# Equal instead of unequal token pieces in the weight-stationary projections of a hybrid SSD and MLA step

## The chip, the cores and the metric

The kernel runs on one core of one Trainium2 chip. The metric is the device time of one execution, in microseconds, lower is better. The core's engines are named as in the profile: PE (TensorE, with PEld for its weight loads), DVE (VectorE), ACT (ScalarE), POOL (GpSimd) and SP (SyncE, which issues most DMAs here).

## The reference

One inference step of two layers, for 1024 prompt tokens and 8 x 8 sample tokens, 1088 tokens of width 1024 in all. The layers are a Mamba-2 SSD layer and a latent attention (MLA) layer, each as h = h + Mixer(RMSNorm(h)). Only the projections that read the normed tokens are touched by the change:

```python
def ssd_mixer(h, conv_buf, ssm_state, w_in, conv_w, ...):
    proj = jnp.einsum('btd,de->bte', h, w_in)          # 1024 -> 2048 + 4096 + 32
    z = proj[..., :SSD_D_INNER]
    xbc = proj[..., SSD_D_INNER:SSD_D_INNER + SSD_CONV_DIM]   # 4096 columns
    xbc, new_buf = causal_conv(xbc, conv_buf, conv_w, conv_b)
    xbc = jax.nn.silu(xbc.astype(F32))
    ...                                                # the scan, gated norm, w_out

def mla_project(h, pos, w_in, ...):
    proj = jnp.einsum('btd,de->bte', h, w_in)
    gate = proj[..., o3:]                              # 1024 columns
    ...
```

The first layer's 4096 columns that go to the convolution, and the second layer's 1024 gate columns, are computed with the weights stationary in PE and the tokens moving.

## The kernel before

**Precision and order.** Each float32 operand is split into a high and a low part, and a product is three matmuls: high x high, low x high, high x low (`pairs` in `proj_piece`). The normed tokens lie transposed in `xh` and `xl` (`hh` and `hl` in the second layer), 8 tiles of 128 features by 1088 tokens.

**Weight-stationary projections.** A block is 128 output columns. `proj_piece` computes one block for one piece of the tokens: 8 feature tiles x 3 matmuls = 24 matmuls accumulate in one PSUM buffer of the tag "pj", of which there are two, and `evac` copies the piece out on ACT. A block has three pieces, taken from the list `TG`. In the first layer `Group.block` does it for 4 blocks in each of 8 groups (32 blocks); its eviction `ev` copies the first two pieces into `raw` (L511) and splits the last one into its prompt tokens (L513) and the 64 sample tokens (L514). Then ACT and DVE do the convolution from `raw` (L524, L528). In the second layer `gate_block` does 8 blocks, evicted through SiLU into `gt` (L994). `TG` also sets the three token groups in which the rows are normed and transposed (`norm_rows`, `norm_cols`, 384, 384 and 320 tokens).

**Around them.** A group's `gates` (the tile `z`, matmuls `pz` at L101 with the tokens stationary) and the scan of the group before (`ssd_chunks` and `ssd_states`) are put between the pieces. In the scan, a chunk's transposes write `trp` (L597 to L600), `cb` is B times C (L628), `py` the product with the decay matrix M (L640), `st` the state. The sample states' product `pv` (L726) shares its PSUM buffer with `cb`; ACT copies half of it to `yo` (L728) and DVE adds the rest (L729). `conv_out` transposes the last conv inputs (`ctp`), and `ssd_dt` makes the step sizes (`dpa`, L410). At the end of the first layer `OutHalf.prep` reads rows of y back into `yta0`, `yta1`, ... (two tiles in turn, even and odd), DVE scales them (L821), PE transposes them into `ytpa` (L829), ACT and DVE split them into `yha` and `yla`, and `ssd_out` multiplies them by the output weights into `poa` (L101), which DVE adds to the residual `xra` (L857).

**What sets the order.** A scheduler lays out all engines' instructions by simulated times, with estimated durations, except where the code pins them; in the second layer's attention PE and POOL are laid out by hand. So the program that results is one fixed order for each engine, in which an instruction waits only for what it needs.

Of the kernel before, what the change touches and what calls it, by code (L numbers as in the profile page):

```python
# [26 lines left out]
HD = 64  # L27
G = 8
TG = [(0, 384), (384, 384), (768, 320)]
TILES = [(i * 128, 128) for i in range(8)] + [(1024, 64)]  # L30
RAW = 3 + SEQ + NB * (NT + 3)
QL, KVL, ROPE, NOPE = 512, 256, 32, 64
# [53 lines left out]
def mm3(nc, out, pairs):  # L86
    n = len(pairs)
    for i, (a, b) in enumerate(pairs):
        nc.tensor.matmul(out, a, b, start=(i == 0), stop=(i == n - 1))  # L89
# [15 lines left out]
def both(xh, xl, i, kk):  # L105
    t0, m = TILES[i]
    a = xh[:, kk, t0 : t0 + m]
    return (a, None, xh[:, kk, t0 : t0 + 128]) if m == 64 else (a, xl[:, kk, t0 : t0 + m], None)
# [111 lines left out]
def rstd_of(k, out, ssq, n):  # L220
    nc = k.nc
    nc.vector.tensor_scalar(out, ssq, 1.0 / n, EPS, op0=ALU.mult, op1=ALU.add)
    m, n = out.shape[0], int(np.prod(out.shape[1:]))
    e = k.nhalf[:m, :n]
    if len(out.shape) == 3:
        e = e.rearrange("p (a b) -> p a b", a=out.shape[1])
    return nc.gpsimd.tensor_tensor(out, out, e, op=ALU.pow)
# [15 lines left out]
def norm_rows(k, gi, load, pool, xbufs):  # L243
    nc = k.nc
    t0, n = TG[gi]
    idx = [i for i, (a, m) in enumerate(TILES) if t0 <= a < t0 + n]
    xs = []
# [3 lines left out]
    for j, i in enumerate(idx):  # L251
        m = TILES[i][1]
        xt = pool.tile([128, D], F32, tag="xt", name=f"xt{i}", bufs=xbufs)
        load(xt, i)
        sq = k.sqp(f"sq{i}")
        with k.tc.issue_after(k.cols[gi - 1][SQ[gi - 1] + j].ins) if gi else nullcontext():
            nc.scalar.activation(sq[:m], xt[:m], AF.Square, accum_out=ssq[:m, j : j + 1])
        xs.append((xt, m, TILES[i][0] - t0))
        k.pow = rstd_of(k, rs[:, j : j + 1], ssq[:, j : j + 1], D)
# [5 lines left out]
def norm_cols(k, gi, xs, wcol, hi, lo, psum):  # L265
    nc = k.nc
    t0, n = TG[gi]
    for d in range(8):
# [18 lines left out]
def norm_steps(k, load, wcol, hi, lo, pool, psum, steps, xbufs, before=None, after=None, tail=False):  # L287
# [6 lines left out]
    for gi in range(3):  # L294
# [13 lines left out]
        if tail and gi == 0:  # L308
            xr, m = k.hr[8]
            k.tc.keep_in_program_order(k.nc.gpsimd.dma_start(k.h_d[TILES[8][0] : T], xr[:m]))  # L310

# [7 lines left out]
def load_w(k, pool, src, nk, ncol, tag, bufs=3, raws=None, rbufs=2, eng=None, sub=0, late=None):  # L319
    raw = load_raw(raws or pool, nk, ncol, rbufs)  # L320
    k.lastload = k.nc.sync.dma_start(raw, src.rearrange("(k p) e -> p k e", p=128))
    hi = pool.tile([128, nk, ncol], F32R, tag=tag + "h", name=tag + "h", bufs=bufs)
    lo = pool.tile([128, nk, ncol], F32R, tag=tag + "l", name=tag + "l", bufs=bufs)
    if late is None:
        split(k, hi, lo, raw, eng, sub)
    else:
        late.append((hi, lo, raw))
    return hi, lo
# [9 lines left out]
def kslices(w, n):  # L338
    return [(w[0][:, kk], w[1][:, kk]) for kk in range(n)]


def proj_piece(k, psum, ws, xh, xl, ci, evac):
    nc = k.nc
    t0, n = TG[ci]
    p = psum.tile([128, 512], F32, tag="pj", name="pj", bufs=PB["pj"])
    pairs = []
    for kk, (hi, lo) in enumerate(ws):
        a, b = xh[:, kk, t0 : t0 + n], xl[:, kk, t0 : t0 + n]
        pairs += [(hi, a), (hi, b), (lo, a)]
    mm3(nc, p[:, :n], pairs)  # L350
    evac(ci, t0, n, p)
# [109 lines left out]
class Group:  # L461
# [34 lines left out]
    def block(self, bi, acc):  # L496
        k, g, nc, wp, rp, gp = self.k, self.g, self.k.nc, self.wp, self.rp, self.gp
        blk = (16 + g, 24 + g, 2 * g, 2 * g + 1)[bi]
        first = g == 0 and bi == 2
        with ExitStack() as es:  # L500
            if first:
                es.enter_context(k.tc.issue_after(k.cols[1][7].ins))
                es.enter_context(k.tc.issue_after(k.xl_dma.ins))
            ws = self.pre.pop(bi, None) or self.weights(bi)
        raw = rp.tile([128, RAW], F32, tag="raw", name=f"raw{g}{bi}", bufs=2)
        smp = raw[:, 3 + SEQ :].rearrange("p (b w) -> p b w", w=NT + 3)
        nc.gpsimd.memset(raw[:, 0:3], 0.0)

        def ev(ci, t0, n, p):
            if ci < 2:  # L510
                nc.scalar.copy(raw[:, 3 + t0 : 3 + t0 + n], p[:, :n])  # L511
            else:
                nc.scalar.copy(raw[:, 3 + t0 : 3 + SEQ], p[:, : SEQ - t0])  # L513
                nc.scalar.copy(smp[:, :, 3:], p[:, SEQ - t0 : n].rearrange("p (b w) -> p b w", w=NT))  # L514

        for ci in range(3):
            if ci == 2:
                nc.gpsimd.tensor_copy(smp[:, :, 0:3], k.convT[:, blk].rearrange("p (b w) -> p b w", w=3))
            proj_piece(k, self.psum, ws, k.xh, k.xl, ci, ev)
            yield  # L520
        nc.gpsimd.tensor_copy(self.ct[:, bi, 0:3], raw[:, SEQ : SEQ + 3])
        nc.gpsimd.tensor_copy(self.ct[:, bi, 3:].rearrange("p (b w) -> p b w", w=3), smp[:, :, NT:])
        n = RAW - 3
        nc.scalar.activation(acc, raw[:, 3:], AF.Identity, bias=k.convb[:, blk : blk + 1],  # L524
                             scale=k.convw[3][:, blk : blk + 1])
        for j in range(3):
            with k.tc.issue_after(self.conv.ins) if self.conv else nullcontext():
                last = nc.vector.scalar_tensor_tensor(acc, raw[:, j : j + n], k.convw[j][:, blk : blk + 1], acc,  # L528
                                                      op0=ALU.mult, op1=ALU.add)
        self.conv = last if g == 0 and bi == 0 else None  # L530
# [18 lines left out]
    def gates(self):  # L549
# [3 lines left out]
        self.z = []  # L553
        for i, (t0, m) in enumerate(TILES):
            if i % 5 == 0:
# [431 lines left out]
def gate_block(k, wp, raws, b):  # L987
    with k.tc.issue_after(k.gts[5].ins) if b in (3, 4) else nullcontext():
        ws = kslices(load_w(k, wp, k.I["mla_w_in"][0][:, 800 + 128 * b : 928 + 128 * b], 8, 128, "wg", 3, raws,
                            eng=k.nc.gpsimd, sub=4), 8)  # L990
    gt = wp.tile([128, T], F32, tag="gt", name=f"gt{b}", bufs=2)

    def ev(ci, t0, n, p):
        k.gts.append(k.nc.scalar.activation(gt[:, t0 : t0 + n], p[:, :n], AF.Silu))  # L994

    for ci in range(3):
        proj_piece(k, k.psum, ws, k.xh, k.xl, ci, ev)
        yield
    k.gst = k.nc.sync.dma_start(k.g_d[b], gt)

# [12 lines left out]
def mla_in(k, right, mid):  # L1013
    tc, nc, I = k.tc, k.nc, k.I
    k.g_d = k.dram.tile([8, 128, T], F32, name="g_d")
    with ExitStack() as st:
# [8 lines left out]
        with k.h0, open_pool(tc, name="h1", bufs=1, side="right") as p0:  # L1025
            k.gts = []
            tc.keep_in_program_order(nc.scalar.preload_act_table_set("silu_and_others"))
            first = [gate_block(k, wg, rw, 0), gate_block(k, wg, rw, 1)]
            norm_steps(k, h_loader(k), k.normc[1], k.xh, k.xl, p0, k.psum, first, 3, tail=True)
            for b in first:  # L1030
                next(b, None)
# [5 lines left out]
        def gate_steps():  # L1037
            for b in range(2, 8):
                for ci, _ in enumerate(gate_block(k, wg, rw, b)):
                    if b > 2:  # L1040
                        next(stage, None)
                    yield
# [1083 lines left out]
```

## Time and profile before

| | us |
|---|---|
| three runs | 1914.87, 1917.70, 1918.49 |
| median | 1917.7 |
| span of the profiled execution | 1915.0 |
| PE busy in it | 1887.4 |
| DVE, ACT, POOL busy | 1208.5, 1101.1, 823.3 |

The span is the profiled execution's time from its first to its last instruction; no other time is known of that execution. A busy PE means that some matmul is under way: matmuls overlap, so that their starts, and not their durations, tell the rate. "Idle before" is the time in which an engine had nothing under way, with the engine and line that ended it.

### The profile page before, as it was taken

How to read it: one execution, taken by the hardware profiler on the slowest of the kernel's cores; microseconds unless marked ns; L12 is line 12 of the kernel's file. 1: busy time of each engine (PE TensorE's matmuls, PEld its weight loads, DVE VectorE, ACT ScalarE, POOL GpSimd, SP SyncE). 2: the span in 40 equal slices, each digit the busy share in tenths (PEclk: the TensorE clock that was granted, in tenths of full speed). 3: DMA queues.
4: the chain of work that ended last, by engine and by line, in shares of the span. 5: the costliest groups of instructions: out<-in, count | busy, mean ns of one | idle time of the engine just before them, and what ended most of it. 6: DMA issues, size and time to landing. Idle time of an engine off the chain costs nothing.

```text
span 1915.0 us, 33672 instructions
## 1 busy us (share of the span) xinstructions
PE 1887.4 (99%) x12023; PEld 1728.1 (90%) x12023; DVE 1208.5 (63%) x2500; ACT 1101.1 (57%) x2528; POOL 823.3 (43%) x1116
## 2 busy tenths in 40 slices
PE   8999999999999999999999999999999999999998
PEld 7999999999999999888788998898888887888887
DVE  5557676757676767765534214566887878666665
ACT  6467666767666666732214323436777777755552
POOL 2447555555655555453004322103443434764551
PEclk9999999999999999999999999999999999999999
DMA  5223323332323232644424662233111112664451
GB/s 165 54 79 91 94 83 94 88 106 83 101 84 99 85 99 78 212 158 175 166 110 133 209 226 75 69 110 95 47 52 41 53 41 58 228 204 142 146 170 37
DMA packets 183967, 212.51 MB, mean 111 GB/s; under 512 B 19148, under 2 KB 147928, under 8 KB 182776
## 3 DMA queue, kind: packets, MB, share of 16 engines
q1 hardware_dynamic: 177304, 185.32, 31.1%
q0 software_dynamic: 6416, 24.91, 3.8%
q8 instruction: 95, 1.56, 0.3%
q14 instruction: 72, 0.59, 0.1%
q10 hardware_dynamic: 80, 0.13, 0.0%
HBM read 151.76 MB, written 58.52 MB: 110 GB/s over the span
## 4 chain that ended last, share of the span: by engine, by line
PE 90%; DMA 3%; DVE 3%; ACT 3%; issue 1%; POOL 0%; SPq 0%; POOLq 0%; DVEq 0%; ACTq 0%
PE pj L89 24%; PE pz L101 8%; PE pq L101 6%; PE pob L101 5%; PE p L101 5%; PE poa L101 4%; PE py L640 3%; PE sc L89 3%; PE o L89 2%; PE sc L1402 2%; PE o L1465 2%; PE o L1467 2%; PE st L1434 2%; PE st L1435 2%; PE st L1436 2%; PE o L1466 2%
## 5 line engine op out<-in xcount | busy, mean ns | idle before, releaser
L89 PE MATMUL pj<-xl,wih 128*128 128x384 f32 (+1 forms) x768 | 255.4, 333 | 0.0
L89 PE MATMUL pj<-xh,wih 128*128 128x384 f32 (+1 forms) x768 | 252.9, 333 | 1.2 <-ACT xh L276 0.8
L89 PE MATMUL pj<-xh,wil 128*128 128x384 f32 (+1 forms) x768 | 252.9, 329 | 0.0
L1448 POOL TENSOR_TENSOR tl<-P,th 128x384 fp32r<-128x384 f32 (+1 forms) x96 | 90.6, 944 | 232.3 <-ACT P L1446 186.6
L528 DVE SCALAR_TENSOR_TENSOR acc<-raw,vec,acc 128x1112 f32<-128x1112 f32 x96 | 141.6, 1476 | 15.3 <-ACT acc L524 14.4
L89 PEld LDWEIGHTS pj<-xh,wih 128*128 128x128 f32 x768 | 143.8, 188 | 2.6 <-ACT xh L276 1.4
L89 PEld LDWEIGHTS pj<-xl,wih 128*128 128x128 f32 x768 | 144.5, 188 | 1.0
L89 PEld LDWEIGHTS pj<-xh,wil 128*128 128x128 f32 x768 | 144.5, 188 | 0.5
L101 PE MATMUL pz<-wih,xh 128*128 128x256 f32 x504 | 143.3, 288 | 1.4 <-ACT z L569 1.4
L101 PE MATMUL pz<-wil,xh 128*128 128x256 f32 (+1 forms) x504 | 139.8, 283 | 0.0
L1445 ACT ACTIVATE th<-st 128x512 fp32r<-128x512 f32 x192 | 94.6, 493 | 66.6 <-PE st L1441 50.9
L101 PE MATMUL pz<-wih,xl 128*128 128x256 f32 x448 | 128.5, 287 | 0.0
L1733 POOL TENSOR_TENSOR kvl<-pgr,kvh 128x256 fp32r<-128x256 f32 x128 | 97.8, 791 | 70.6 <-ACT kvh L1731 70.3
L635 ACT ACTIVATE M<-M,tok 128x128 f32<-128x128 f32 (+1 forms) x288 | 90.4, 386 | 51.4 <-DVE M L631 51.2
L136 DVE TENSOR_TENSOR wil<-wraw,wih 128x512 fp32r<-128x512 f32 x88 | 74.4, 851 | 38.2 <-ACT wih L130 31.7
L101 PEld LDWEIGHTS pz<-wih,xh 128*128 128x128 f32 x504 | 95.9, 190 | 2.3 <-ACT z L569 1.8
L1446 ACT ACTIVATE P<-st 128x512 f32<-128x512 f32 x192 | 93.5, 487 | 0.0
L101 PEld LDWEIGHTS pz<-wil,xh 128*128 128x128 f32 (+1 forms) x504 | 92.8, 184 | 0.1
L101 PE MATMUL p<-w,oh 128*128 128x512 f32 (+3 forms) x304 | 88.8, 386 | 0.6 <-DVE h L1983 0.6
L616 POOL TENSOR_TENSOR xdd<-xsT,tok 128x256 f32<-128x256 f32 x64 | 50.0, 781 | 86.4 <-ACT xsT L602 83.3
L101 PEld LDWEIGHTS pz<-wih,xl 128*128 128x128 f32 x448 | 85.4, 191 | 0.7
L1448 DVE TENSOR_TENSOR tl<-P,th 128x512 fp32r<-128x512 f32 x96 | 72.1, 752 | 18.9 <-ACT P L1446 18.7
(830 smaller groups left out, 6212.5 us busy)
## 6 DMA issues: line engine op xcount, KB each, us to landing
wraw<-in_ssd_w_in SPq DMA_DIRECT2D x92, 256.0 KB
M<-acs_d SPq DMA_DIRECT2D x64, 256.0 KB
s<-in_state_ssm SPq DMA_DIRECT2D x32, 256.0 KB
y_d<-y SPq DMA_DIRECT2D x64, 128.0 KB
out_s_ssm<-s SPq DMA_DIRECT2D x32, 256.0 KB
q_d<-qt SPq DMA_DIRECT2D x32, 192.0 KB
qp<-q_d SPq DMA_DIRECT2D x8, 768.0 KB
wraw<-in_ssd_w_out SPq DMA_DIRECT2D x10, 512.0 KB
```

Of the source, the lines that this page charges most:

```text
L89: nc.tensor.matmul(out, a, b, start=(i == 0), stop=(i == n - 1))
L101: nc.tensor.matmul(o, a, b, start=(j == 0), stop=(j == len(ops) - 1))
L136: return (eng or nc.vector).tensor_tensor(lo, src, hi.bitcast(F32), op=ALU.subtract)
L528: last = nc.vector.scalar_tensor_tensor(acc, raw[:, j : j + n], k.convw[j][:, blk : blk + 1], acc, op0=ALU.mult, op1=ALU.add)
L616: nc.gpsimd.tensor_tensor(v3(xdd), v3(xsT), hb(2), op=ALU.mult)
L635: nc.scalar.activation(M[:m, h, :m], M[:m, h, :m], AF.Exp, bias=tk[:, 0, 4 * g + h : 4 * g + h + 1])
L640: nc.tensor.matmul(py[:m, h * 64 : h * 64 + 64], M[:m, h, :m], xsT[:m, h * 64 : h * 64 + 64], start=True, stop=True)
L1402: nc.tensor.matmul(ps[:, :n], qh[:96, 128 * i : 128 * i + 128], kh[:96, 512 * c : 512 * c + n], start=True, stop=True)
L1445: nc.scalar.activation(th[:, :n], ps[:, :n], AF.Exp, scale=SCALE)
L1446: nc.scalar.activation(P[:, :n], ps[:, :n], AF.Exp, scale=SCALE)
L1448: eng.tensor_tensor(tl[:, :n], P[:, :n], th[:, :n].bitcast(F32), op=ALU.subtract)
L1733: nc.gpsimd.tensor_tensor(rl[:, j], raw[:, j], rh[:, j].bitcast(F32), op=ALU.subtract)
```

## The change

`proj_piece` takes the list of pieces as an argument. The first layer passes `PG`, the gates pass `PG2`. The norm groups keep `TG`. The numbers of pieces, blocks and matmuls stay.

```diff
 TG = [(0, 384), (384, 384), (768, 320)]
+PG = ((0, 368), (368, 368), (736, 352))
+PG2 = ((0, 376), (376, 360), (736, 352))
...
-def proj_piece(k, psum, ws, xh, xl, ci, evac):
+def proj_piece(k, psum, ws, xh, xl, ci, evac, parts):
     nc = k.nc
-    t0, n = TG[ci]
+    t0, n = parts[ci]
...
-            proj_piece(k, self.psum, ws, k.xh, k.xl, ci, ev)
+            proj_piece(k, self.psum, ws, k.xh, k.xl, ci, ev, PG)
...
-        proj_piece(k, k.psum, ws, k.xh, k.xl, ci, ev)
+        proj_piece(k, k.psum, ws, k.xh, k.xl, ci, ev, PG2)
```

The list of instructions on each engine stays the same but for the widths; their order, which the scheduler makes, changes from the first block to the gates on all engines. It is untouched in the attention that follows. Three places, with the order before and after (the changed kernel's lines have numbers two higher, and names carry the number of the buffer).

*The end of the first layer, DVE.* Before; `yta1` and `yta2` are rows of y for the second and third token tile of the output projection, `wraw` its weights, and the names with 6 and 7 belong to the scans of the last two groups:

```order
L636 TENSOR_TENSOR M7_0_10410<-M7_0_10410,cb7_0_10408 128x512
L113 TENSOR_TENSOR z75_10203<-z75_10203,pz_10348 64x256
L821 TENSOR_SCALAR yta2_10705<-yta2_10705,yrsa_10323 128x256 x4
L663 TENSOR_TENSOR y6_8_10286<-y6_8_10286,z65_8883 64x256
L136 TENSOR_TENSOR BTl7_0_10397<-trp7_0_10390,BTh7_0_10396 128x128
L774 SCALAR_TENSOR_TENSOR xl_99<-wraw_10382,vec_154,xh_98 128x8x128
```

and eleven rows on from L821:

```order
L663 TENSOR_TENSOR y7_0_10429<-y7_0_10429,z70_9914 128x256
L821 TENSOR_SCALAR yta1_10512<-yta1_10512,yrsa_10323 128x256 x4
L136 TENSOR_TENSOR sl7_800_10465<-s0p7_800_10459,sh7_800_10464 128x512
L631 TENSOR_TENSOR M7_1_10562<-M7_1_10562,negu_69 128x512
L631 TENSOR_TENSOR M7_2_10647<-M7_2_10647,negu_69 128x512
L857 TENSOR_TENSOR xra0_10484<-xra0_10484,poa00_10486 128x512
```

After:

```order
L776 SCALAR_TENSOR_TENSOR xl_99<-wraw_10386,vec_154,xh_98 128x8x128
L700 TENSOR_TENSOR xf7_80_10447<-x3p7_80_10439,tok3_78 96x256
L823 TENSOR_SCALAR yta1_10512<-yta1_10512,yrsa_10323 128x256 x4
L633 TENSOR_TENSOR M7_1_10562<-M7_1_10562,negu_69 128x512
L705 TENSOR_TENSOR x37_80_10449<-xf7_80_10447,x37_80_10449 32x256
L708 TENSOR_TENSOR b37_80_10452<-x3p7_80_10439,b37_80_10452 32x128
L664 TENSOR_TENSOR y7_0_10429<-py7_0_10418,xD7_0_10406 128x256
L649 COPY S7_1_10427<-st7_0_10423 128x256
L138 TENSOR_TENSOR sl7_800_10465<-s0p7_800_10459,sh7_800_10464 128x512
L665 TENSOR_TENSOR y7_0_10429<-y7_0_10429,z70_9914 128x256
L823 TENSOR_SCALAR yta2_10705<-yta2_10705,yrsa_10323 128x256 x3
L859 TENSOR_TENSOR xra0_10484<-xra0_10484,poa00_10486 128x512
```

The scaling of yta2 moved from ahead of yta1 to behind it, and in SP's queue its read moved behind that of yta1 in the same way.

*The same stage, PE.* Before, from the last rows ahead of the transposes of yta0 to the first `poa` (between the two pieces stand eight more `pz` matmuls):

```order
L628 MATMUL cb6_8_10271<-xs60_8139 64x64
L829 MATMUL ytpa00_10334<-ident_58,yta0_10326 128x128 x4
L829 MATMUL ytpa01_10341<-ident_58,yta0_10326 128x128 x4
L101 MATMUL pz_10348<-wih_9898,xh_98 128x256
L101 MATMUL pz_10348<-wil_9899,xh_98 64x256
```

and at the end of that stretch:

```order
L101 MATMUL pz_10348<-wih_9910,xh_98 128x256
L640 MATMUL py6_8_10281<-xsT6_8_10267,M6_8_10273 64x64 x4
L628 MATMUL cb7_0_10408<-acc70_9057 128x128
L101 MATMUL poa00_10486<-xh_98,yha0_10332 128x512
L101 MATMUL poa00_10486<-xl_99,yha0_10332 128x512
```

After:

```order
L103 MATMUL pz_10348<-wil_9911,xh_98 64x256
L103 MATMUL pz_10348<-wih_9910,xh_98 128x256
L831 MATMUL ytpa00_10334<-ident_58,yta0_10326 128x128 x4
L831 MATMUL ytpa01_10341<-ident_58,yta0_10326 128x128 x4
L642 MATMUL py6_8_10281<-xsT6_8_10267,M6_8_10273 64x64 x4
L630 MATMUL cb7_0_10408<-acc70_9057 128x128
L103 MATMUL poa00_10486<-xh_98,yha0_10332 128x512
L103 MATMUL poa00_10486<-xl_99,yha0_10332 128x512
```

The transposes ytpa moved behind the eleven `pz` matmuls, so that only py and cb stand between them and the first poa.

*The end of the first block, ACT.* Before; `raw00` and `raw01` take the last pieces of the first two blocks, `wih_699` and `wih_1188` are high parts of the next weights:

```order
L276 ACTIVATE xh_98<-xtp2_7_498,vec_154 128x320
L513 COPY raw00_259<-pj_506 128x256
L514 COPY raw00_259<-pj_506 128x8x8
L513 COPY raw01_287<-pj_534 128x256
L514 COPY raw01_287<-pj_534 128x8x8
L524 ACTIVATE acc00_258<-raw00_259,vec_154 128x1112
L524 ACTIVATE acc00_258<-raw01_287,vec_154 128x1112
L130 CAST wih_699<-wraw_697 128x512
```

After:

```order
L278 ACTIVATE xh_98<-xtp2_7_498,vec_154 128x320
L132 CAST wih_699<-wraw_697 128x512
L515 COPY raw00_259<-pj_506 128x288
L516 COPY raw00_259<-pj_506 128x8x8
L515 COPY raw01_287<-pj_534 128x288
L516 COPY raw01_287<-pj_534 128x8x8
L526 ACTIVATE acc00_258<-raw00_259,vec_154 128x1112
L526 ACTIVATE acc00_258<-raw01_287,vec_154 128x1112
```

The cast of wih_699 moved ahead of the four copies out of PSUM. In the later groups the order differs from the one before in each, and groups 2 and 4 are now laid out alike, as are 3 and 5: between the last `pv` of a group and its last `cb` (chunk 7) stood 38 `pz` matmuls in groups 2 to 5, and stand 43 in groups 2 and 4 and 34 in groups 3 and 5. In groups 3 and 5 the first four matmuls of the next conv block (`pj`) now stand ahead of the transposes `trp` of the next group's first chunk, which stood ahead of them. `dpa` stands two `pj` matmuls later.

## The prediction

> **What bounds the kernel now.** I read the page first (busy times), then the busy times by stretch, the groups of instructions by form, the timeline of TensorE (PE) for the spacing of matmuls, and the waits of PE.
>
> ```profile
> span 1915.0 us, 33672 instructions
> PE 1887.4 (99%) x12023; PEld 1728.1 (90%) x12023; DVE 1208.5 (63%) x2500; ACT 1101.1 (57%) x2528; POOL 823.3 (43%) x1116
> ```
>
> PE is busy for 99% of the span, while the next engine, VectorE (DVE), is busy for 63%. So the time is the sum of PE's matmul spacings plus the little that it waits. The stretches below are the first layer's groups, its output projection, and the gates:
>
> ```profile
> 60.00:755.00 695.00, 692.00 (x5060) 681.39 (x5059) 463.41 (x744) 455.94 (x1119) 376.95 (x567) 1.00 0.30 88
> 755.00:1027.00 272.00, 268.75 (x1501) 225.61 (x1499) 150.56 (x288) 106.06 (x235) 78.52 (x105) 1.00 0.46 157
> 1027.00:1140.00 113.00, 112.22 (x702) 108.90 (x701) 31.72 (x53) 42.57 (x83) 38.28 (x53) 1.00 0.61 212
> ```
>
> The first number after the comma is PE's busy time. From 60 to 1140 us, where all the changed matmuls but the first few pieces stand, PE is busy for 1072.97 of 1080 us. No stretch here is held by a load or by another engine for long. The granted clock is 1.00 in all three.
>
> **The spacing of a matmul by its width.** The duration of one (0.34 us at 384 columns in the rows below) is a latency: matmuls overlap. What counts is from start to start, read in three clean runs, first and last row of each (start and duration in us):
>
> ```profile
> 1061.67 0.34 PE L89 MATMUL pj<-hl,wgh 128*128 128x384 f32 x1
> ...
> 1069.65 0.34 PE L89 MATMUL pj<-hh,wgl 128*128 128x384 f32 x1
> ...
> 1120.80 0.31 PE L89 MATMUL pj<-hh,wgh 128*128 128x320 f32 x1
> ...
> 1124.17 0.31 PE L89 MATMUL pj<-hh,wgl 128*128 128x320 f32 x1
> ...
> 385.89 0.28 PE L101 MATMUL pz<-wil,xh 128*128 128x256 f32 x1
> ...
> 390.21 0.28 PE L101 MATMUL pz<-wil,xh 128*128 128x256 f32 x1
> ```
>
> The runs hold 47, 24 and 37 matmuls, so 46, 23 and 36 spacings: 7.98/46 = 173.5 ns at 384 columns, 3.37/23 = 146.5 at 320, 4.32/36 = 120.0 at 256. The slope is (173.5 - 146.5)/64 = 0.422 ns a column above 320 and (146.5 - 120.0)/64 = 0.414 below: nearly a straight line, with a fixed part of some 11 ns a matmul.
>
> **Term 1, the matmuls: 0.** The number of matmuls stays and every three pieces still hold 1088 columns. By the line, 368 columns take 173.5 - 16 x 0.422 = 166.7 ns, 352 take 160.0, 376 take 170.1 and 360 take 163.4. Three pieces took 2 x 173.5 + 146.5 = 493.5 ns for each weight tile; now 2 x 166.7 + 160.0 = 493.4 in the first layer and 170.1 + 163.4 + 160.0 = 493.5 in the gates. The first layer has 32 blocks of 24 weight tiles, 768 such sums, and the gates 192. If the bend of the line (0.414 against 0.422) fell all on the new widths, a sum would move by 0.4 ns, so 0.4 us in all to either side. I take 0.
>
> **Term 2, the evictions: 0.** ScalarE (ACT) copies a piece out of PSUM; columns are minimum, median and maximum in ns:
>
> ```profile
> L511 ACT COPY raw<-pj x64: 454/479/503, 24.2 to 749.5; 128x384 f32<-128x384 f32 x64
> L513 ACT COPY raw<-pj x32: 355/367/391, 48.2 to 755.2; 128x256 f32<-128x256 f32 x32
> L514 ACT COPY raw<-pj x32: 209/221/249, 48.5 to 755.4; 128x64 f32<-128x64 f32 x32
> ```
>
> That is (479 - 367)/128 = 0.875 ns a column, so a 368 piece takes 465 ns and the last piece's prompt part, now 288 columns, 395. A block took 2 x 479 + 367 + 221 = 1546 ns and takes 2 x 465 + 395 + 221 = 1546. What hides it is the next piece in the other of the two "pj" buffers, 24 x 160 ns = 3.84 us of matmuls; without that cover the last piece's copies would cost 28 ns more a block, 0.9 us over 32 blocks. I take 0. The gates' SiLU evictions go the same way. Their last piece and the first layer's begin at column 736 instead of 768 and so also read 32 columns of the second norm group, which is transposed before the third: no new wait.
>
> **Term 3, the new order.** The scheduler moved instructions on every engine from the first block to the gates. Each keeps its kind and number, so what can move is PE's waiting. The waits of PE from 60 to 1140 us (total in us, times, longest; six of ten rows):
>
> ```profile
> PE pz L101 <- ACT z L569: 1.4, 2, 0.7
> PE cb L628 <- DVE yo L729: 1.1, 3, 0.4
> PE trp L597 <- DVE yla L136: 1.0, 1, 1.0
> PE ctp L536 <- POOL ct L522: 1.0, 1, 1.0
> PE poa L101 <- DVE xra L857: 0.6, 1, 0.6
> PE dpa L410 <- DVE dta L404: 0.5, 1, 0.5
> ```
>
> The six sum to 5.6 us, and the four others stand below dpa's 0.5 each, so the whole is 5.6 to 7.6 us; I go on with 6.6. No order can gain more than that here by taking waits away, but for shorter pauses that the overlap hides.
>
> *End of the first layer.* The rows of before:
>
> ```profile
> 796.34 1.61 DVE L821 TENSOR_SCALAR yta<-yta,yrsa 128x256 f32<-128x256 f32 x4 [1.88 <-DMA yta<-y_d]
> ...
> 804.50 1.61 DVE L821 TENSOR_SCALAR yta<-yta,yrsa 128x256 f32<-128x256 f32 x4
> ...
> 808.66 0.47 PE L101 MATMUL poa<-xh,yha 128*128 128x512 f32 x1 [0.59 <-DVE xra L857]
> ...
> 810.37 0.33 PE L597 MATMUL trp<-ident,acc 128*128 128x128 f32 x1 [1.01 <-DVE yla L136]
> ```
>
> DVE waits 1.88 us for a tile that it scales too early (yta2) and spends 1.61 us on it, then does yta1, and is late for PE twice, 0.59 + 1.01 us. After the change yta1 comes first, so DVE is up to 1.88 + 1.61 = 3.49 us less behind there: both waits go, -1.6 us at most, 0 at least if DVE falls behind elsewhere; I take the whole. Against it, the transposes ytpa of yta0 come later, with only py and cb between them and the first poa; before, 11 more matmuls (11 x 0.12 = 1.3 us) stood there. poa needs ACT's cast and then DVE's subtraction. Those may now show as a wait, 0 to 1.3 us, and I take 0.5. yta2 is read behind yta1 now, and its transposes stand behind most of the 48 matmuls of tile 1; nobody waits. Together -1.1.
>
> *cb in groups 2 to 5.* PE waits for the PSUM buffer that yo frees:
>
> ```profile
> 292.31 0.28 PE L101 MATMUL pz<-wil,xh 128*128 128x256 f32 x1
> 292.95 0.49 PE L628 MATMUL cb<-acc 128*128 128x128 f32 x2 [0.36 <-DVE yo L729]
> ```
>
> Beyond the overlap it is 292.95 - 292.31 - 0.12 = 0.52 us, since the gate matmul ahead would hold PE for 0.12, and it comes three times, in groups 2, 3 and 4. In groups 2 and 4 now 43 gate matmuls stand ahead of cb instead of 38, 5 x 0.12 = 0.6 us of cover, and ACT's copy of yo is no longer behind y's squares: both waits go, -1.0. In groups 3 and 5 there are 34, 0.5 us less cover, partly made good by the same move on ACT: +0.25 each. Bounds -1.6 (all three gone) and +1.0 (both longer by the full 0.5 us and nothing gone); I take -0.5.
>
> *dpa* stands two matmuls later: 2 x 0.167 of its 0.5 us wait, -0.3.
>
> *End of the first block.* ACT now casts the next weights ahead of the copies that free the first "pj" buffer:
>
> ```profile
> L130 ACT CAST wih<-wraw 128x512 fp32r<-128x512 f32 x92 | 55.9, 616 | 45.4 <-PE pj L89 30.0 <-DMA wraw<-in_ssd_w_in 15.3
> ...
> 48.22 0.37 ACT L513 COPY raw<-pj 128x256 f32<-128x256 f32 x1 [1.72 <-PE pj L89]
> ...
> 48.76 0.45 PE L89 MATMUL pj<-xh,wih 128*128 128x384 f32 x1 [0.29 <-ACT raw L514]
> ```
>
> ACT had been idle for 1.72 us, so a cast, of 616 ns by its group's row, fits if its weights have landed: 0, or +0.6 if they land late. I take +0.2.
>
> *Group starts.* In groups 3 and 5 the first four conv matmuls now follow the gates directly, ahead of the transposes, on weights that ACT and DVE have only just split. I take +0.3 for each, +0.6, between 0 and 1.2 (twice the 616 ns of a cast).
>
> The sum is 0 + 0 - 1.1 - 0.5 - 0.3 + 0.2 + 0.6 = -1.1 us: 1913.9 us against the profiled execution's span of 1915.0. The median of the three runs is 1917.7, 2.7 above that span, so the forecast for the median is 1916.6. That is no change that can be measured: 0.2%, 3.8 us, is about what the runs can tell from none.
>
> **Rivals.** (a) *The array works in blocks of 32 columns.* Every width of these projections was a multiple of 64 before, so no row above speaks against it. 368, 376 and 360 would cost as 384, and the sum of three would be 1120 columns: 32 x 0.422 = 13.5 ns for 960 sums, +13.0 us, 1930.7. It decides if the 368 rows start 173 ns apart and not 167. For blocks of 16 only the gates lose, 16 columns in 192 sums, +1.3 us. The Trainium skill's page "TensorE: Matmul & The Clock Gate" (Step-by-step: what each phase is for) says that one column of the moving operand enters each cycle, so that throughput follows the column count alone; by that rule this rival is impossible and term 1 stays 0. The trace agrees at 256, 320 and 384 columns, where the slope is even; no run here yet shows a width between. (b) *New waits.* The order was laid out by estimated times, and PE can arrive early at products of ACT and DVE all over the seven group changes: the longest wait of the kind (pz on ACT) is 0.7 us. One at each of the seven and at the layer's end would add 8 x 0.7 = 5.6 us: 1923. It needs six such waits beyond those of before to pass 0.2%. (c) *The waits go.* If the list above vanished whole, 6.6 us would go: 1911. It must lose more than half, 3.8 us, to be faster by 0.2%; the four places that I followed give 3.4 at their best, and ctp and pz, 2.4 us, are open.
>
> **Numbers.** The forecast has 0.54, (c) 0.25, (a) 0.05 and (b) 0.16. So faster 0.25, same 0.54, slower 0.21. The range reaches from 1908, (c) with some short pauses gone as well, to 1926, past (b); (a) is left out.
>
> **What would show it.** In the changed kernel's profile the 368 and 352 matmuls should start 167 and 160 ns apart, and ACT's copies of 368 and 288 columns take 465 and 395 ns. PE's waits on yla and xra should be gone, and the waits of cb be seen in groups 3 and 5 alone. PE's share should stay at 99%. Wrong would be a spacing off the line by 5 ns, which is worth 4 us and more, or waits of PE from 60 to 1140 us that sum to under 3 or over 10 us.

## The result: 1.26% slower, and the profile after

The changed kernel took 1940.98 us in the median (1937.54 to 1942.53, 4 runs) against 1916.28 us (1914.14 to 1918.49, 4 runs) for the kernel before: a ratio of 1.0126, 95% interval 1.0111 to 1.0140. The forecast was no measurable change, 1916.6 us, with 1926.0 as the upper end of the range, so it missed.

The first lines of the page of the changed kernel:

```profile
span 1935.8 us, 33636 instructions
PE 1896.0 (98%) x12023; PEld 1731.0 (89%) x12023; DVE 1199.9 (62%) x2500; ACT 1100.2 (57%) x2528; POOL 828.6 (43%) x1116
```

The span grew by 20.8 us, PE's busy time by only 8.6. The same three stretches as in the prediction, the first made 20 us longer and the others moved by as much (the same columns: length, then PE, PEld, DVE, ACT and POOL busy, clock, DMA share, GB/s):

```profile
60.00:775.00 715.00, 701.94 (x5093) 687.41 (x5092) 456.31 (x746) 457.68 (x1125) 388.10 (x571) 1.00 0.30 86
775.00:1047.00 272.00, 265.65 (x1460) 221.07 (x1459) 147.81 (x284) 102.73 (x227) 74.31 (x101) 1.00 0.48 157
1047.00:1160.00 113.00, 112.21 (x693) 108.89 (x692) 32.69 (x54) 42.82 (x80) 38.88 (x53) 1.00 0.61 208
```

In the first stretch, the groups of the first layer, PE is idle for 715.00 - 701.94 = 13.1 us, where it was 695.00 - 692.00 = 3.0. In the second, the output projection, it idles 6.4 us (3.3 before), in the gates 0.8 as before. The stretches are cut by time and don't hold quite the same matmuls (5093 for 5060 in the first). Followed by instruction, the last conv matmul starts 16.1 us later than before (at 769.50 for 753.40) and the last one of the output projection 20.7 us later (at 1046.48 for 1025.80). The clock is a rounded mean: it reads 1.00 in all three, but in the first it hides a short drop to half, which the last section shows. Which waits these are, from the waits of PE in the same range (total in us, times, longest):

```profile
PE st L91 <- POOL xddl L138: 8.9, 8, 2.5
PE cb L630 <- DVE M L638: 2.0, 1, 2.0
PE pv L728 <- DVE sl L138: 1.6, 4, 0.9
PE cb L630 <- DVE yo L731: 1.3, 3, 0.7
PE st L91 <- ACT xddh L132: 1.0, 2, 0.7
PE sn L735 <- POOL bb L710: 1.0, 2, 0.5
PE poa L103 <- ACT yha L132: 0.9, 1, 0.9
PE pv L728 <- ACT sh L132: 0.8, 1, 0.8
PE poa L103 <- DVE xra L859: 0.7, 1, 0.7
```

The first row was not in the list before at all: in the scan, PE waits for `xddl`, the low part of the decayed inputs, which POOL makes for the state product `st`. The waits leave out what the overlap hides. So I also added up, for each kind of matmul, the time from the start of the matmul ahead to its own start, over the whole execution: these sums grew by 20.8 us, `st` by 12.9, `pj` 4.1, `pv` 3.0, `cb` 2.8, and everything else together fell by 2.1.

**The largest place.** It comes three times alike, in chunk 5 of the scans of groups 1, 3 and 5. First POOL at this chunk of group 1 in the kernel before, by its timeline (start, duration):

```profile
270.89 1.13 POOL L616 TENSOR_TENSOR xdd<-xsT,tok 128x256 f32<-128x256 f32 x1 [1.37 <-ACT xsT L602]
271.98 0.61 POOL L626 TENSOR_TENSOR xD<-xsT,dsk 128x256 f32<-128x256 f32 x1
272.55 0.73 POOL L136 TENSOR_TENSOR xddl<-xdd,xddh 128x256 fp32r<-128x256 f32 x1
```

DVE beside it, in the same timeline:

```profile
270.17 1.38 DVE L528 SCALAR_TENSOR_TENSOR acc<-raw,vec,acc 128x1112 f32<-128x1112 f32 x1 [0.84 <-ACT acc L524]
271.58 0.28 DVE L729 TENSOR_TENSOR yo<-yo,pv 32x128 f32<-32x128 f32 x1
271.88 0.69 DVE L735 TENSOR_TENSOR s<-s,sn 128x512 f32<-128x512 f32 x1
...
273.29 1.35 DVE L528 SCALAR_TENSOR_TENSOR acc<-raw,vec,acc 128x1112 f32<-128x1112 f32 x1
```

POOL at this chunk in the changed kernel's timeline:

```profile
269.46 1.34 POOL L618 TENSOR_TENSOR xdd<-xsT,tok 128x256 f32<-128x256 f32 x1 [1.66 <-ACT xsT L604]
270.77 2.11 POOL L628 TENSOR_TENSOR xD<-xsT,dsk 128x256 f32<-128x256 f32 x1
272.84 2.03 POOL L138 TENSOR_TENSOR xddl<-xdd,xddh 128x256 fp32r<-128x256 f32 x1
```

DVE beside it:

```profile
267.65 0.28 DVE L731 TENSOR_TENSOR yo<-yo,pv 32x128 f32<-32x128 f32 x1
267.96 0.69 DVE L737 TENSOR_TENSOR s<-s,sn 128x512 f32<-128x512 f32 x1
268.96 1.38 DVE L530 SCALAR_TENSOR_TENSOR acc<-raw,vec,acc 128x1112 f32<-128x1112 f32 x1 [0.32 <-ACT acc L526]
...
271.05 1.35 DVE L530 SCALAR_TENSOR_TENSOR acc<-raw,vec,acc 128x1112 f32<-128x1112 f32 x1
272.33 0.67 DVE L638 TENSOR_TENSOR M<-M,cb 128x512 f32<-128x512 f32 x1
272.93 1.36 DVE L530 SCALAR_TENSOR_TENSOR acc<-raw,vec,acc 128x1112 f32<-128x1112 f32 x1
```

And PE, which had come to this matmul at 272.4:

```profile
274.93 0.58 PE L91 MATMUL st<-xddl,BTh 128*128 128x256 f32 x1 [2.39 <-POOL xddl L138]
```

Before, DVE's two operations `yo` and `s` (0.97 us) stood between the first and the second step of a convolution, and POOL did xD and xddl in that gap, in 0.61 and 0.73 us. In the new order `yo` and `s` go ahead of the first step. The steps move together, and xD and xddl each fall on one: 2.11 and 2.03 us for the same work. Each ends about half a microsecond after the step beside it (272.88 after 272.40, 274.87 after 274.29), as if it did next to nothing while the step ran. Over all 192 operations of this kind (xdd, xD, xddl), 57 now stand beside a convolution step and take 43.8 us more than alone; before, 41 took 26.7 us more.

The Trainium skill, "SBUF — State Buffer" (SBUF: two separate sides; Who interferes with whom), says that a DVE instruction with two inputs in SBUF and a GpSimd instruction that reads SBUF contend for one shared read port, as an exclusive lock: whichever starts first gets it for the whole instruction, and the other fully blocks. The convolution step (raw and acc) has two such inputs, and the rows agree. They do not agree with the page's sentence that whoever starts first gets the port: by the profile xD started 0.28 us ahead of its step, and it was xD that stood. Whether the recorded start is the start of POOL's reads is not known.

**A wait of another kind.** `cb`'s 2.0 us for M comes in the scan of the last group, which runs beside the output projection. M stands on DVE behind the scaling of a tile of y, and DVE had idled 2.51 us for the read of that tile:

```profile
877.85 1.97 DVE L823 TENSOR_SCALAR yta<-yta,yrsa 128x256 f32<-128x256 f32 x4 [2.51 <-DMA yta<-y_d]
879.74 0.68 DVE L638 TENSOR_TENSOR M<-M,cb 128x512 f32<-128x512 f32 x1
```

### The profile page after: what moved, and what is told of

Read it like the earlier page. It is cut to its first block, busy times and chain, and to the rows that moved or that the text cites. A ratio compares the mean times of both kernels' runs of the same rounds, so it can differ in the third digit from the quotient of the medians.

```text
span 1935.8 us, 33636 instructions
## 1 busy us (share of the span) xinstructions
PE 1896.0 (98%) x12023; PEld 1731.0 (89%) x12023; DVE 1199.9 (62%) x2500; ACT 1100.2 (57%) x2528; POOL 828.6 (43%) x1116
## 4 chain that ended last, share of the span: by engine, by line
PE 82%; DMA 5%; ACT 4%; DVE 3%; POOL 3%; issue 2%; SPq 0%; POOLq 0%; DVEq 0%; ACTq 0%
PE pj L91 20%; PE pz L103 7%; PE pq L103 6%; PE pob L103 5%; PE p L103 5%; PE poa L103 4%; DMA M<-acs_d 3%; PE sc L91 3%; PE o L91 2%; PE py L642 2%; PE sc L1404 2%; PE o L1467 2%; PE o L1469 2%; PE st L1436 2%; PE st L1438 2%; PE st L1437 2%
## 5 line engine op out<-in xcount | busy, mean ns | idle before, releaser
L91 PE MATMUL pj<-xl,wih 128*128 128x368 f32 (+1 forms) x768 | 255.6, 333 | 0.0
L91 PE MATMUL pj<-xh,wih 128*128 128x368 f32 (+1 forms) x768 | 254.1, 335 | 1.3 <-ACT raw L516 0.7
L91 PE MATMUL pj<-xh,wil 128*128 128x368 f32 (+1 forms) x768 | 253.7, 330 | 0.0
L138 DVE TENSOR_TENSOR wil<-wraw,wih 128x512 fp32r<-128x512 f32 x88 | 70.5, 806 | 50.8 <-ACT wih L132 50.3
```

Of the source, the lines that this page charges most:

```text
L138: return (eng or nc.vector).tensor_tensor(lo, src, hi.bitcast(F32), op=ALU.subtract)
```

## The experiments

Theory A: the new order costs the time, above all by POOL's work standing beside DVE's convolution steps (A1). Theory B: the widths themselves cost it. An order can be kept while widths change, because every piece lies in a PSUM buffer of 512 columns: the program is laid out with one list of pieces, and then the operands of the 2880 matmuls and the copies out of PSUM are given other offsets and lengths in place.

**Old order, new widths, and the reverse.**

```diff
+    recut(nc, OLD, NEW)      # after the layout: pj matmuls and evictions get new offsets and widths
     r = run_bass_kernel_spmd(nc, [arrays], core_ids=[0])
```

> The order of the kernel before on every engine, with the new widths put in place of the old ones (368, 368, 352 and 376, 360, 352). Theory A, the new order costs the time: only the spacing of the matmuls is left. In the changed kernel three pieces of the first layer take 2 x 167.7 + 162.6 = 498.0 ns for a weight tile against 2 x 174.5 + 146.5 = 495.5 before, and of the gates 502.2 against 494.4, so 768 x 2.5 + 192 x 7.8 = 3.4 us: 1916.3 + 3.4 = 1919.7 us, and PE waits for st on POOL's xddl nowhere for over 0.5 us. Theory B, the widths cost the time (evictions and matmuls that don't fit each other any more): about 1941 us, with the order of before.

> The order of the changed kernel on every engine, with the old widths (384, 384, 320 in both layers). Theory A, the new order costs the time: 1941.0 - 3.4 = 1937.6 us, the waits of st on xddl stay at 2.4 to 2.7 us in three places. Theory B, the widths cost it: about 1916 us.

| | widths before | widths after |
|---|---|---|
| order before | 1 | 1919.76 us, 1.0005 (0.9994 to 1.0016) |
| order after | 1939.75 us, 1.0121 (1.0101 to 1.0140) | 1940.98 us, 1.0126 (1.0111 to 1.0140) |

Ratios are to the kernel before in the same session, which took 1918.56 us beside the two new cells and 1916.28 beside the changed kernel. The order alone makes 1.21%, the widths alone +0.05% (1.0 us, between -1.1 and +3.1), which is no difference that can be told. The first of PE's waits with the old widths in the new order shows the same place:

```profile
PE st L91 <- POOL xddl L138: 8.5, 5, 2.5
```

Theory B has fallen. Theory A's 3.4 us for the spacing lies just above the upper end of what was measured, 3.1: 1919.7 us was met, but beside a kernel before that took 1918.56 and not 1916.3.

**POOL without the steps beside it.** The nine steps at the three places, cut to 64 columns, so that this part of the convolution is left out:

```diff
+    narrow(nc)               # after the layout: acc<-raw steps of raw23, raw43, raw63: 1112 -> 64 columns
     r = run_bass_kernel_spmd(nc, [arrays], core_ids=[0])
```

> The changed kernel and its order; nine steps of the convolution on DVE (three each of the last blocks of groups 2, 4 and 6, which run beside POOL's work for chunk 5 of the scans of groups 1, 3 and 5) work on 64 of their 1112 columns, so that part of the convolution is left out. Theory A1, POOL is slowed by DVE's work beside it: xddl of these three chunks takes 0.73 us instead of 2.03, and xD 0.61 instead of 2.11; the three waits of PE for st, 2.5 us each, go: 1941.0 - 7.5 = 1933.5 us. Theory A2, POOL gets its input late, or is held by its own queue: its two operations keep 2 us each and the time stays at 1941.

Measured: 1933.19 us, ratio to before 1.0076 (1.0058 to 1.0095). POOL's timeline at the same place:

```profile
269.88 0.61 POOL L618 TENSOR_TENSOR xdd<-xsT,tok 128x256 f32<-128x256 f32 x1 [1.66 <-ACT xsT L604]
270.45 0.62 POOL L628 TENSOR_TENSOR xD<-xsT,dsk 128x256 f32<-128x256 f32 x1
271.02 0.74 POOL L138 TENSOR_TENSOR xddl<-xdd,xddh 128x256 fp32r<-128x256 f32 x1
```

The operations take 0.62 and 0.74 us again although POOL waits as long for its first input (1.66 us for xsT, as in the changed kernel), and the time fell by 7.8 us, or 9.6 by the ratios (1.0126 to 1.0076), where the three waits are worth 7.5 from start to start. Between the two profiles the sum for `st` fell by just these 7.5 us. A2, late inputs or POOL's own queue, has fallen: the steps beside them make the slowness.

**xddl ahead of xD.** The same three places with the two exchanged in POOL's queue, and nothing left out:

```diff
 L618 xdd1_5<-xsT1_5,tok
+L138 xddl1_5<-xdd1_5,xddh1_5
 L628 xD1_5<-xsT1_5,dsk
-L138 xddl1_5<-xdd1_5,xddh1_5
```

> The changed kernel and its order, except that in chunk 5 of the scans of groups 1, 3 and 5 POOL does xddl ahead of xD, for which PE doesn't wait. Theory A1 (POOL slowed by DVE beside it, and xddl behind a slowed xD): xddl starts when ACT's xddh is there, 271.25 instead of 272.84 us, and still takes about 2.0, so it ends some 1.6 us earlier; three waits of 2.5 us become 0.9: 1941.0 - 4.8 = 1936.2 us. If xddl's place behind xD doesn't matter, the time stays at 1941.

Measured: 1932.81 us, 1.0074 (1.0056 to 1.0092), 8.2 us less than the changed kernel (10 by the ratios) where 4.8 were expected. POOL's timeline:

```profile
271.20 1.67 POOL L138 TENSOR_TENSOR xddl<-xdd,xddh 128x256 fp32r<-128x256 f32 x1 [0.52 <-ACT xddh L132]
272.84 1.81 POOL L628 TENSOR_TENSOR xD<-xsT,dsk 128x256 f32<-128x256 f32 x1
```

Both are still slow, but xddl ends at 272.87 instead of 274.87 us, a little earlier than expected (1.67 and not 2.0 us), and no wait of st for POOL is over 0.6 us now. From start to start `st` lost 5.1 us between the two profiles, near the 4.8 expected. The rest was not traced; some 4 us of it can be the granted clock, whose median over the runs is 0.998 here and 0.996 in the changed kernel (the last section has the estimate). So the place of a slowed operation that nobody waits for, ahead of one that PE waits for, made most of those waits.

**How much of the whole is POOL beside DVE.** All 96 convolution steps on DVE cut to 64 columns, in the changed kernel and in the kernel before, so that most of the convolution is left out of both:

```diff
-                        getattr(a, "memref", "")[:6] in ("raw23_", "raw43_", "raw63_") for a in i.ins):
+                        getattr(a, "memref", "").startswith("raw") for a in i.ins):
```

> The changed kernel and its order; all 96 steps of the convolution on DVE work on 64 of their 1112 columns, so that most of the convolution is left out and DVE has some 100 us less to do. Theory P, POOL slowed by these steps is the main cost of the new order: beside the 7.5 us of the three places, the three half-microsecond waits for xddl in chunk 4 and the 0.9 us wait in group 7 go, and this kernel comes within some 5 us of the next one (the order of before, cut alike): about 1925 us or less. Theory R, the rest of the loss is waits of another kind (pv on DVE's sl, cb on DVE's M and yo, which only follow from what stands ahead of what): it stays at 1929 to 1933 us, over 10 us above the next one.

> The kernel before and its order, with the same 96 steps cut to 64 columns. It is the floor to compare with: PE has few waits there, and those for DVE and POOL (cb on yo 1.1 us, ctp on POOL 1.0, the steps' end) can shrink: 1914 to 1919 us by both theories.

Measured: 1926.06 us, 1.0047 (1.0030 to 1.0065), and 1915.47 us, 0.9991 (0.9981 to 1.0001). The two orders lay 24.7 us apart and now lie 10.6 us apart in one session. So the steps account for some 14 us of the loss, 7.5 of it at the three places; the rest, 10.6 us, is of another kind: with the steps cut, xdd, xD and xddl take only 0.6 us in all more beside them than alone. Some 3 us of it can be the granted clock (0.9975 in the median against 0.999; estimate in the last section). Neither theory hit: P gave 5 us, R over 10 with the time at 1929 or more. What remains of PE's waits in the changed order, the first rows:

```profile
PE st L91 <- ACT xddh L132: 1.8, 3, 1.2
PE cb L630 <- DVE M L638: 1.5, 1, 1.5
PE pv L728 <- DVE sl L138: 1.5, 4, 0.7
```

These look like waits that follow from what stands ahead of what on ACT and DVE; none of them was tested. From start to start the two profiles differ by 12.6 us, with `st` 4.8, `pj` 3.6 (the spacing of the new widths among it), `pv` 1.8 and `cb` 1.2. Cutting the steps also frees DVE of some 100 us, so the 14 us are not the contention's alone. What makes up the rest stays open.

**Another order for nearly the same work.**

```diff
-PG = ((0, 368), (368, 368), (736, 352))
-PG2 = ((0, 376), (376, 360), (736, 352))
+PG = ((0, 384), (384, 352), (736, 352))
+PG2 = TG
```

> Other widths in the first layer (384, 352, 352; the gates as before), and the order that the scheduler makes for them. In that order DVE's s and yo stand again between two convolution steps ahead of chunk 5 in every group, as in the kernel before, and the third step stands later. Theory A1: xD and xddl of chunk 5 then take 0.6 to 1.1 us and no wait of 2.5 us for st remains: at most 1941.0 - 7.5 = 1933.5 us, and down to 1918 if nothing else was lost. If the widths that differ from multiples of 64 were to blame, it would be near 1941 like the changed kernel.

Measured: 1923.35 us, 1.0031 (1.0017 to 1.0046), as A1 expected (at most 1933.5); xD and xddl of chunk 5 take 0.61 and 0.74 us in groups 1 to 5. Of the waits for xddl, 0.9 us are left, two of at most 0.6; `cb` on M, 2.0 us, stays. Pieces that differ from the changed kernel's by 16 columns in the first layer, and by 8 to 32 in the gates, gave an order 17.6 us better, and one that is still slower than the one before.

**The mend in the source, for both kernels.** The code holds xD behind xddl in the first and last group. Held in all:

```diff
-        with k.tc.issue_after(behind.ins) if not smp and g in (0, G - 1) else nullcontext():
+        with k.tc.issue_after(behind.ins) if not smp else nullcontext():
```

> The changed kernel with xD held behind xddl in all groups in the source (so far in the first and the last alone), and the order that the scheduler then makes. On DVE the three convolution steps now lie around chunk 5's xdd, xD and xddl in all five groups 1 to 5, without s and yo between, as in groups 1, 3 and 5 of the changed kernel. If it is the place of xddl behind a slowed xD that counts, no wait of st passes 1 us and the time is 1928 to 1935 us, as with the three exchanged by hand (1932.8). If a crowded DVE costs by itself, five places instead of three cost 2.5 us each: 1941 + 5 = 1946 us.

> The kernel before with xD held behind xddl in all groups in the source, in the order that the scheduler then makes. DVE has s and yo between the convolution steps in all five groups, and PE waits for xddl nowhere there, so there is nothing to win: 1914 to 1920 us. If the wait for xddl is what a scheduler's new order puts in by chance, it can be slower, up to 1925.

Measured: the changed kernel with it 1941.37 us, 1.0123 (1.0106 to 1.0140); the kernel before with it 1921.48 us, 1.0018 (1.0008 to 1.0028). The first is a miss. The single waits for xddl came out nearly as expected, none over 1.1 us where 1 us was the bound, but the scheduler made a new order around the pin, with more waits of the other kinds. The first rows of PE's waits:

```profile
PE st L91 <- POOL xddl L138: 4.6, 7, 1.1
PE cb L630 <- DVE yo L731: 4.0, 6, 0.9
PE pv L728 <- DVE sl L138: 3.9, 9, 0.7
PE st L91 <- ACT xddh L132: 3.8, 6, 0.7
```

An exchange by hand in a standing order gained 8 us; the same exchange given to the scheduler as a rule gained nothing, since all else moved too. In the kernel before, where no such wait was to be had, the rule lost 0.2%.

**The widths in one sweep.** The order of before, with the 32 blocks cut in 16 ways:

> The order of the kernel before; the 32 blocks of the first layer are cut in 16 different ways (two blocks each), with pieces of 288 to 512 columns, and the gates in 376, 360, 352. By the straight line of the prediction (11 ns + 0.422 ns a column) the matmuls start 139.5 ns apart at 336, 156 at 344, 160 at 352, 163 at 360, 167 at 368, 170 at 376, 180 at 400, 187 at 416, 200 at 448. By the spacing that the changed kernel shows (352 at 158 or at 167 in different runs, 360 at 166.4, 376 at 173), widths that are no multiple of 64 lie 1 to 3 ns above the line, and multiples of 64 on it. By blocks of 32 columns, all widths from 353 to 384 would take 173.

One run, 1923.82 us. Mean spacing between neighbouring matmuls of one width (longer pauses left out; 13 of the 27 widths), against the prediction's line:

| columns | 320 | 336 | 344 | 352 | 360 | 366 | 368 | 376 | 384 | 386 | 400 | 416 | 448 |
|---|---|---|---|---|---|---|---|---|---|---|---|---|---|
| line, ns | 146 | 153 | 157 | 160 | 163 | 166 | 167 | 170 | 173 | 174 | 180 | 187 | 200 |
| measured, ns | 146.2 | 153.3 | 157.8 | 162.2 | 166.4 | 166.8 | 168.1 | 173.2 | 174.8 | 178.3 | 180.7 | 188.3 | 202.8 |

The block rival is refuted: 366 columns would take 173 ns in blocks of 32. (336 lies on the line, 14 ns above what the expectation gives for it there, which was a slip of mine in the sum.) Nor is "multiples of 64 on the line, others above" the rule: 336 is on it, 448 is 2 ns above. What holds for these 16 cuts is that no width beats the line by over 0.5 ns in the mean, and that 386 columns lie 4 ns above it.

No version that does the whole work beat the kernel before.

## Why the prediction was wrong, point by point

**The step that failed is term 3, and in it the sentence "Each keeps its kind and number, so what can move is PE's waiting".** Kind and number stayed, but not the durations, and from them came waits at places that the prediction did not follow: PE's waits from 60 us to the end of the gates went from the 6.6 us that it started from to 19.5, where its places together gave -1.1. Of POOL's operations, xddl went from 56.5 to 64.8 us in all, xD from 49.4 to 57.5. The group of xddl before (form, count, busy, mean ns, idle before):

```profile
L136 POOL TENSOR_TENSOR xddl<-xdd,xddh 128x256 fp32r<-128x256 f32 x64 | 56.5, 883 | 40.2 <-ACT xddh L130 36.4 <-PE cb L628 3.2 <-DVE BTl L136 0.5
```

and in the changed kernel:

```profile
L138 POOL TENSOR_TENSOR xddl<-xdd,xddh 128x256 fp32r<-128x256 f32 x64 | 64.8, 1012 | 35.9 <-ACT xddh L132 35.2 <-DVE BTl L138 0.5
```

The warning stood in the profile of before: a mean of 883 ns over a median of 738, with single ones up to 1.82 us.

- *The places.* I followed those where PE already waited, and added two where the order of PE itself looked worse. The cost arose where PE had not waited before, through an exchange on DVE (`yo` and `s` against a convolution step) and its effect on POOL. `st`, 12.9 of the 20.8 us, is in no term.
- *Rival (b), new waits,* is what happened, and its price was wrong: I took 0.7 us, the longest wait for ACT, eight times, though the list of before has two of 1.0 us. Three were 2.5 us, and there were some twenty smaller ones. A longest wait of an order that was kept bounds nothing for another order.
- *End of the first layer,* forecast -1.1: the wait on yla went, that on xra stayed at 0.7 us, and the open end of it, poa on ACT's yha, was 0.9 us (0.5 taken). `cb` waited 2.0 us for M there, which I had not seen: the very thing that I had followed for two tiles, DVE held up by a tile of y that it scales too early, came back at a later one. By the list that is +2.0.
- *cb on yo,* forecast -0.5: I counted the groups in two ways. The 43 and 34 gate matmuls are numbered by the scan's group, but the three waits of before lie in the scans of groups 1, 2 and 3, not 2, 3 and 4 (292.95 us is 20 us behind chunk 5 of group 1, at 273). Beyond the matmul ahead they cost 0.52 us each; now 0.17 is left in group 1 and 0.12 in 2, and it is 0.44 in 3 and in 5. That is -0.4 in sum, so the -0.5 came near by luck. A new wait of 0.7 us at the layer's end makes it +0.2 by the list.
- *dpa,* forecast -0.3, was -0.1; *the end of the first block,* forecast +0.2, was +0.5 (0.45 to 0.91 us from start to start); at the *group starts,* forecast +0.6, no wait appeared.
- *Term 2, evictions,* was right: 466 and 393 ns at 368 and 288 columns, 465 and 395 forecast.
- *Term 1, matmuls,* was off a little in size, not in the time that can be told: in the changed kernel 368 columns took 167.7 ns in the mean, 352 took 162.6, 360 took 166.4 and 376 took 173.1, where the line gave 166.7, 160.0, 163.4 and 170.1. That makes 768 x 2.5 + 192 x 7.8 ns = 3.4 us there; the widths alone measured +0.05% in the old order (-0.06 to +0.16%). Rival (a) is refuted, but the number of columns alone does not set the spacing either (last section).
- *The clock* was taken as 1.00 for the new order too. In the runs it was lower than in the kernel before, by an estimate worth some 6 us (last section).
- *Two slips that change no chance:* the rivals' times count from the median of 1917.7 and the forecast from 1916.6; and the best of the places followed is, by their own bounds, 1.6 + 1.6 + 0.3 = 3.5 and not 3.4.
- *The signs named ahead:* waits of PE that sum to over 10 us were named as what would show the prediction wrong, and they sum to 19.5.

## What to carry to other kernels

Where a scheduler orders the work, any change of a size makes a new order, and in a kernel whose PE is 99% busy a new order is most of what is measured: here five orders of nearly the same work took from 1916 to 1941 us, and the one before was the best of them. Separate the two by keeping the order and changing the sizes in place, before crediting or blaming the sizes. When comparing orders, look not only at what each engine waits for but at which long DVE operations with two SBUF inputs (here the convolution steps) stand beside POOL's, and in a standing order put what PE waits for first in POOL's queue. Look at the clock by short windows too, since a mean over a stage hides a drop of 3 us.

## What the runs showed of the hardware

**DVE's step can be held up too.** In one place POOL started first and both operations were longer (Sl 0.92 us, where 0.74 is the median); in chunk 4 of group 1 of the changed kernel, POOL's timeline:

```profile
256.07 0.92 POOL L138 TENSOR_TENSOR Sl<-S,Sh 128x256 fp32r<-128x256 f32 x1
256.95 1.80 POOL L138 TENSOR_TENSOR xddl<-xdd,xddh 128x256 fp32r<-128x256 f32 x1
```

and DVE's:

```profile
256.32 1.85 DVE L530 SCALAR_TENSOR_TENSOR acc<-raw,vec,acc 128x1112 f32<-128x1112 f32 x1
```

The step took 1.85 instead of 1.35 us, half a microsecond more, while Sl held on until 256.99; then xddl stood until the step ended at 258.17 and needed 0.58 us more. At the largest place xD had started first too and the step kept its 1.35 us, so the recorded start alone does not tell which of the two is held up.

**Between the widths seen before, a matmul's spacing is mostly not on the line, and it has more than one value.** The same 352 columns, in two runs of the changed kernel, first and last row of each (24 and 22 matmuls):

```profile
68.95 0.33 PE L91 MATMUL pj<-xh,wih 128*128 128x352 f32 x1
...
72.60 0.32 PE L91 MATMUL pj<-xh,wil 128*128 128x352 f32 x1
...
647.58 0.32 PE L91 MATMUL pj<-xh,wil 128*128 128x352 f32 x1
...
651.07 0.33 PE L91 MATMUL pj<-xh,wil 128*128 128x352 f32 x1
```

3.65/23 = 158.7 ns in the one and 3.49/21 = 166.2 in the other, at the same granted clock; within the first the spacings run 155, 160, 157, 162 and repeat, within the second 166, 167, 167. 376 columns alternate between 170 and 177 ns. What sets the phase was not tried.

**PE's clock fell to half behind long waits.** The same columns as for the stretches above, over 3.5 us of the changed kernel and of the old widths in the new order:

```profile
274.60:278.10 3.50, 3.17 (x15) 3.17 (x16) 0.71 (x2) 1.84 (x4) 1.25 (x3) 0.51 0.07 19
478.60:482.10 3.50, 3.50 (x20) 3.50 (x19) 0.41 (x2) 3.47 (x5) 2.13 (x7) 0.51 0.03 7
```

In the first, PE has just waited 2.39 us for xddl. Its matmuls of 256 columns then start 0.21 us apart (276.59, 276.80), where it was 0.12 ahead of the wait (272.14, 272.26). Each drop lasts some 3.4 us, so by an estimate, half of that, it takes 1.7 us of PE's work. From 60 to 1160 us the twelve kept profiles have ten waits of PE over 2.0 us; at six of them the clock falls, between 0.5 us before the wait's end and 0.9 us after it. Two more drops stand there behind shorter waits (1.09 us with xD held in the changed kernel, 0.82 us in the sweep). The kernel before has neither such a wait nor a drop in this stretch. Why some waits have a drop and others not was not tried.

The four runs of the changed kernel had mean clocks of 0.998, 0.996, 0.995 and 0.996 and took 1937.54, 1941.69, 1942.53 and 1940.27 us; fourteen runs of the kernel before in a later session had 0.999 in the median. A thousandth of the span is 1.9 us, so by an estimate the clock makes some 6 of the 24.7 us between the medians. It fits that the profiled run, the one of 0.998, was the shortest, and that the profiles lie only 20.8 us apart.
